# Two later norms by stream between halves of output tiles, and four modulation blocks on VectorE instead of TensorE

## The chip, the core and the metric

The kernel runs on one core of a Trainium2 chip. TensorE (PE in the profile) multiplies matrices into PSUM, VectorE (DVE) and ScalarE (ACT) work elementwise, and SyncE (SP) issues nearly all weight loads. The metric is the device time of one execution in microseconds (us).

## The reference

Two layers of a diffusion transformer on 256 latent tokens (stream 1) and 256 context tokens (stream 0), width 1024, in fp32. Every sublayer is "modulated norm, mixer, gated residual"; the six modulation vectors of a layer come from one conditioning vector for each stream.

```python
s_lat = jax.nn.silu(c)
s_ctx = jax.nn.silu(c_ctx)[None]
for l in range(DEPTH):
    sh_m, sc_m, g_m, sh_f, sc_f, g_f = jnp.split(s_lat @ w_mod[l] + b_mod[l], 6, axis=-1)
    csh_m, csc_m, cg_m, csh_f, csc_f, cg_f = jnp.split(s_ctx @ w_mod[l] + b_mod[l], 6, axis=-1)
    u = modulate(h, norm_mix[l], sh_m, sc_m)      # rms_norm(h) * (1 + scale) + shift
    uc = modulate(hc, norm_mix[l], csh_m, csc_m)
    ...   # y, yc = hybrid_mixer (l = 0) or ssd_mixer (l = 1)
    h = h + g_m[:, None] * y
    h = h + g_f[:, None] * conv_ffn(modulate(h, norm_ffn[l], sh_f, sc_f), ...)
    if need_ctx:      # layer 0 only
        hc = hc + cg_m[:, None] * yc
        hc = hc + cg_f[:, None] * conv_ffn(modulate(hc, norm_ffn[l], csh_f, csc_f), ...)
```

The hybrid mixer is a neighbourhood attention beside a gated linear recurrence (hgrn), then one output projection. The ssd mixer is a state-space scan with its own projections. `conv_ffn` is two up-projections, a convolution of width 3, a gelu gate and a down-projection.

## The kernel before

**Layout.** Activations lie as 128 features by 512 tokens: columns 0 to 255 are stream 0, 256 to 511 stream 1. `h` holds the residual in eight such tiles (k = 0 to 7). A matrix product is made of two fp32r pieces for each operand: `xhi` and `xlo` for the activations, `whi` and `wlo` for a weight. `mm3` (L141) issues three matmuls for each k, so a projection of 128 outputs (`proj`, L146) is 24 matmuls over eight k.

**Weights.** `wsplit` (L126) loads a 128x1024 block `raw` by SyncE, rounds it on ScalarE to `whi` (L135) and takes the rest on VectorE as `wlo` (L137). All three have four buffers. `behind` can tie the next splits behind given instructions.

**Modulations** are made in two ways. In *blocks* on TensorE (`mod_block`, L187), eight matmuls for each block, at the end of a batch two transposes and a reduction (`mod_finish`, L199 to L201); `queue` and `fetch` load the next block, two tiles `wv`. In *units* on VectorE (`vec`, L269): a unit is one row block of 128 outputs, two `junk` operations over 128x1024 whose sum goes to `dots`, one for each stream. `vec_fetch` (L252) loads up to three units ahead, each into a tile `wv`. Units and blocks share the five buffers of `wv`. Eight units fill one of the six chunks of a layer.

**Stages.** `hybrid`: first norm, two recurrence pairs, `attention` (head pairs: scores L684 and L685 on PE, bias L689, row maximum L691, exponent on ScalarE, reciprocal L694 and scaling L695 on VectorE, transposes L698, values L704, then `mhi`, `mlo` at L397 and L398), output projection `wo0` of eight tiles n (the last in two stream halves), each with `residual` (L390, `h`) and `sumsq` (L313 `nsq`, L317 `nacc`). Its products over k = 4 to 7 need `xhi`, `xlo`, those over k = 0 to 3 need `mhi`, `mlo`. Then `ffn(0)`: `norm_mod`, 22 features f with projections a (`ps_a`) and v (`ps_s`), in three chunks each followed by eight down-projection tiles m, the last again in halves. Layer 1: `norm_mod`, `ssd` (projections, L837 to L1010), `ffn(1)` on stream 1 alone.

**A later norm** (`norm_mod`, L381) issues a block, the sums over partitions (L324), a block, the rsqrt chain (`rsv` L328, Ln and Exp on ScalarE L288, `rst` L330 and L331, `nr` L332), the broadcast (L340), a block, and then for each k and stream `nt` (L374, VectorE), `xhi` (L376, ScalarE), `xlo` (L377, VectorE).

**What sets the order.** The code gives dependences and a program order; a list scheduler then fixes the instruction order of each engine at build time, from a model of its own. An engine executes its instructions in that order. Moving code in one place can so move instructions of other stages.

Of the kernel before, what the change touches and what calls it, by code (L numbers as in the profile page):

```python
# [43 lines left out]
class Net:  # L44
# [274 lines left out]
    def norm_r(self, ps, t0, n, meanwhile):  # L319
# [5 lines left out]
        between = meanwhile(last)  # L325
        r = self.w.tile([P, 4], F32, tag="nr", bufs=1, name=self.nm("nr"))[:, :nt]
# [6 lines left out]
        if not self.ps0:  # L333
            self.behind = [(self.squared, done.ins), (), (), ()]
# [7 lines left out]
        meanwhile(last)  # L342
# [24 lines left out]
    def norm_u(self, l, which, k, r, xhi, xlo, streams, pool):  # L367

        nc = self.nc
        t = pool.tile([P, T], F32, tag="nt", bufs=2, name=self.nm("nt"))  # L370
# [41 lines left out]
    def ffn(self, l, streams, xhi, xlo, last):  # L412
# [3 lines left out]
        with tc.tile_pool(name=f"ffn{l}", bufs=1) as p:  # L416
            self.norm_mod(l, 1, xhi, xlo, streams, p)
            for c, (f0, nf) in enumerate(FF_CHUNKS):
                hh = p.tile([P, NK, n], F32R, tag="hh", name=self.nm("hh"))
                hl = p.tile([P, NK, n], F32R, tag="hl", name=self.nm("hl"))  # L420
                for j in range(nf):
                    f = f0 + j
                    pa, pv = self.ps_a()[:, :n], self.ps_s()[:, :n]
                    self.proj(pa, self.i["wup"][l, f], xhi, xlo, toks=toks)
                    self.proj(pv, self.i["wup"][l, NFF + f], xhi, xlo, toks=toks)
                    if f == 1:
                        self.flush()
# [7 lines left out]
                for m in range(NK):  # L435
                    final = not last and c == len(FF_CHUNKS) - 1

                    for part in ((st,) for st in streams) if final and m == NK - 1 else (streams,):
                        o = (part[0] - streams[0]) * S
                        ps = self.ps_a()[:, :S * len(part)]  # L440
                        if part[0] == streams[0]:
                            w = self.wsplit(self.i["wdn"][l, m, :, f0:f0 + nf], [P, nf, P])
# [682 lines left out]
```

## Time and profile before

| | us |
|---|---|
| median of three runs (lowest to highest) | 1235.34 (1234.79 to 1238.77) |
| the profiled execution | 1236.18 |
| its span in the trace | 1234.4 |
| PE busy | 1205.3 (98%) |
| VectorE busy | 924.7 (75%) |
| ScalarE busy | 589.8 (48%) |

The profiled execution has 1.78 us around its span. Stages in the trace, us from its start: recurrence to about 210, attention to 335, output projection to 363.5, ffn(0) from 370.3 to 740, ssd to 1038, ffn(1) to the end. A busy share of PE counts pipelined matmuls one behind the other; what matters is when the next one starts. The granted clock is 1.00 in the stretches shown below.

### The profile page before, as it was taken

The numbers are of one execution on the slowest core, as the hardware profiler recorded it, in microseconds if no ns is written. First come the engines' busy times: TensorE is split into PE (matmuls) and PEld (weight loads), VectorE is DVE, ScalarE is ACT, GpSimd is POOL, SyncE is SP. The second block draws the span as 40 slices with busy tenths as digits, with TensorE's granted clock in tenths as the row PEclk, the third lists the DMA queues.
The fourth block names the chain that finished last, engine by engine and source line by source line (L and its number), as shares of the span: only waits on it lengthen the run. The fifth ranks groups of instructions, "written<-read, shape, count | busy, mean of one in ns | idle before, by whom it ended". The sixth has DMA issues, their size and how long they took to land.

```text
span 1234.4 us, 19131 instructions
## 1 busy us (share of the span) xinstructions
PE 1205.3 (98%) x7519; PEld 981.4 (80%) x7519; DVE 924.7 (75%) x1596; ACT 589.8 (48%) x915; POOL 0.2 (0%) x4
## 2 busy tenths in 40 slices
PE   5999999999999999999999999999999999999998
PEld 3687787766678888888888887878777798999998
DVE  4799999777569999984344457598989786766675
ACT  4554545787545331233133336556363644645452
POOL 0000000000000000000000000000000000000000
PEclk9999999999999999999999999999999999999999
DMA  9852636313055667762323233445344245565663
GB/s 375 311 180 74 221 102 175 129 56 124 13 161 183 204 217 223 222 201 76 111 91 96 83 112 130 151 144 171 104 152 129 93 135 156 182 186 181 189 183 106
DMA packets 55097, 189.35 MB, mean 153 GB/s; under 512 B 7136, under 2 KB 10848, under 8 KB 53728
## 3 DMA queue, kind: packets, MB, share of 16 engines
q1 hardware_dynamic: 51984, 185.17, 47.0%
q10 hardware_dynamic: 3024, 2.97, 0.8%
q8 instruction: 59, 0.97, 0.3%
q14 instruction: 30, 0.25, 0.1%
HBM read 187.00 MB, written 1.11 MB: 152 GB/s over the span
## 4 chain that ended last, share of the span: by engine, by line
PE 85%; DVE 6%; issue 2%; ACT 1%; DMA 0%; DVEq 0%; ACTq 0%
PE a L144 51%; PE s L144 16%; PE b L704 1%; PE s L161 1%; PE s L162 1%; PE s L163 1%; DVE junk L269 1%; PE b L997 1%; PE b L970 1%; PE b L1002 1%; DVE Q L519 1%; PE s L684 1%; PE b L698 1%; PE s L685 1%; DVE K L519 1%
## 5 line engine op out<-in xcount | busy, mean ns | idle before, releaser
L135 ACT CAST whi<-raw 128x1024 fp32r<-128x1024 f32 (+1 forms) x234 | 241.0, 1032 | 345.3 <-PE a L144 276.9
L137 DVE TENSOR_TENSOR wlo<-raw,whi 128x1024 fp32r<-128x1024 f32 (+1 forms) x234 | 280.5, 1199 | 101.4 <-ACT whi L135 99.8
L144 PE MATMUL a<-xhi,wlo 128*128 128x512 f32 (+1 forms) x740 | 268.9, 370 | 3.6 <-ACT va L639 1.9
L144 PE MATMUL a<-xhi,whi 128*128 128x512 f32 (+1 forms) x740 | 270.8, 366 | 0.0
L144 PE MATMUL a<-xlo,whi 128*128 128x512 f32 (+1 forms) x740 | 258.7, 367 | 2.8 <-DVE xlo L377 2.8
L144 PEld LDWEIGHTS a<-xhi,wlo 128*128 128x128 f32 x740 | 139.0, 188 | 31.3 <-issue 4.1
L144 PEld LDWEIGHTS a<-xlo,whi 128*128 128x128 f32 x740 | 137.4, 188 | 31.5 <-issue 4.6
L144 PEld LDWEIGHTS a<-xhi,whi 128*128 128x128 f32 x740 | 139.3, 188 | 24.7 <-issue 2.9
L269 DVE SCALAR_TENSOR_TENSOR junk<-wv,rows 128x1024 f32<-128x1024 f32 x128 | 156.2, 1221 | 1.9
L144 PE MATMUL s<-xhi,wlo 128*128 128x512 f32 (+1 forms) x376 | 128.4, 341 | 0.0
L144 PE MATMUL s<-xhi,whi 128*128 128x512 f32 (+1 forms) x376 | 128.2, 341 | 0.0
L144 PE MATMUL s<-xlo,whi 128*128 128x512 f32 (+1 forms) x376 | 121.5, 341 | 0.0
L144 PE MATMUL a<-hh,whi 128*128 128x256 f32 (+1 forms) x359 | 120.1, 335 | 0.0
L144 PE MATMUL a<-hh,wlo 128*128 128x256 f32 (+1 forms) x359 | 113.1, 335 | 0.0
L144 PE MATMUL a<-hl,whi 128*128 128x256 f32 (+1 forms) x359 | 112.5, 336 | 0.0
L390 DVE SCALAR_TENSOR_TENSOR h<-a,modT,h 128x256 f32<-128x256 f32 x90 | 40.7, 480 | 69.5 <-PE a L144 69.4
L144 PEld LDWEIGHTS s<-xhi,wlo 128*128 128x128 f32 x376 | 70.5, 188 | 9.5 <-issue 0.4
L144 PEld LDWEIGHTS s<-xhi,whi 128*128 128x128 f32 x376 | 70.6, 188 | 9.5 <-issue 0.4
L144 PEld LDWEIGHTS s<-xlo,whi 128*128 128x128 f32 x376 | 69.2, 188 | 9.0
L144 PEld LDWEIGHTS a<-hh,whi 128*128 128x128 f32 x359 | 67.5, 188 | 7.7
L144 PEld LDWEIGHTS a<-hl,whi 128*128 128x128 f32 x359 | 65.7, 188 | 8.2 <-DVE hl L398 0.5
L144 PEld LDWEIGHTS a<-hh,wlo 128*128 128x128 f32 x359 | 66.0, 188 | 7.8
(339 smaller groups left out, 1793.9 us busy)
## 6 DMA issues: line engine op xcount, KB each, us to landing
raw<-in_wup SPq DMA_DIRECT2D x88, 512.0 KB, 4.0
wv<-in_wmodT SPq DMA_DIRECT2D x64, 512.0 KB, 4.4
raw<-in_win SPq DMA_DIRECT2D x41, 512.0 KB, 3.8
raw<-in_wdn SPq DMA_DIRECT2D x32, 448.0 KB, 3.4
raw<-in_wo SPq DMA_DIRECT2D x24, 512.0 KB, 3.7
wm<-in_wmod SPq DMA_DIRECT2D x8, 1024.0 KB, 10.9
wv<-in_wmod SPq DMA_DIRECT2D x16, 512.0 KB, 4.4
raw<-in_wdn SPq DMA_DIRECT2D x16, 512.0 KB, 3.7
```

The source lines that it names most:

```text
L135: nc.scalar.copy(hi, raw)
L137: nc.vector.tensor_tensor(out=lo, in0=raw, in1=hi.bitcast(F32), op=ALU.subtract)
L144: self.last_mm = self.nc.tensor.matmul(ps, w, x, start=(first and i == 0), stop=(last and i == 2))
L161: mm(ps, xhi[:, k, tok], wlo[:, kk, :], start=(k == 0), stop=False)
L162: mm(ps, xhi[:, k, tok], whi[:, kk, :], start=False, stop=False)
L163: mm(ps, xlo[:, k, tok], whi[:, kk, :], start=False, stop=(k == NK - 1))
L269: nc.vector.scalar_tensor_tensor(out=self.junk, in0=w, scalar=1.0, in1=self.rows[:, s], op0=ALU.mult, op1=ALU.mult, accum_out=self.dots[:, ...
L390: self.nc.vector.scalar_tensor_tensor(out=self.h[:, n, s * S:(s + 1) * S], in0=ps[:, off:off + S], scalar=self.mod(l, chunk, n, s), in1=se ...
L519: mul = lambda o, t: nc.vector.tensor_tensor(out=o, in0=o, in1=t, op=ALU.mult)
L684: nc.tensor.matmul(ps, qs[rows, e, tok], kl[rows, :w], start=True, stop=False)
L685: nc.tensor.matmul(ps, qs[:, e, tok], ks[:, e, :w], start=False, stop=True)
L698: nc.tensor.transpose(pt[:, b * P:(b + 1) * P], pr[:, b * P:(b + 1) * P], self.ident)
```

## The change

Three things change, and the modulations computed are the same.

1. In `wo0` and in the last chunk of ffn(0), tiles 6 and 7 are both taken by stream: 6 and 7 of stream 0, the norm of stream 0 (`norm_stream`), 6 and 7 of stream 1, the norm of stream 1. The first four projections behind (f = 0, 1 of ffn(0)) or the first two (`wdt` and `win1[16]` of ssd) are taken as stream 0 of all and then stream 1 of all (`proj_streams`), as matmuls of 256 columns.
2. Chunk 2 of layer 1 is added to the vector units: 48 units (with those before, 144 `junk`) in place of 40 (128). Of the eight TensorE blocks four remain; they are queued at the end of ssd and run in the norm of ffn(1) (three) and at f = 1 there; the transposes of the last come at f = 2.
3. With no block in a norm, `behind` ties the first two weight splits after a stream's norm to nothing and the third and fourth to its `nr`.

```diff
@@ -331,7 +331,8 @@
         nc.vector.tensor_tensor(out=t, in0=t, in1=v, op=ALU.mult)
         done = nc.vector.scalar_tensor_tensor(out=r, in0=t, scalar=1.5, in1=r, op0=ALU.add, op1=ALU.mult)
         if not self.ps0:
-            self.behind = [(self.squared, done.ins), (), (), ()]
+            late = (self.squared, done.ins)
+            self.behind = [late, (), (), ()] if meanwhile else [late, late, (), ()]
         prs = [self.ps_b()[:, :S] for _ in range(nt // 2)] if self.ps0 else [self.ps_b()[:, :n]]
         with self.after([between] if between else ()):
             for b in range(nt):
...
@@ -378,6 +380,20 @@
                                            op0=ALU.add, op1=ALU.subtract)
         return u
 
+    def norm_stream(self, l, which, st, xhi, xlo):
+
+        r = self.norm_r(self.ps_b(), st * S, S, None)
+        for k in range(NK):
+            self.norm_u(l, which, k, r, xhi, xlo, (st,), self.w)
+
+    def proj_streams(self, jobs, xhi, xlo):
+
+        splits = [self.wsplit(src, [P, NK, P]) for _, src in jobs]
+        for st in STREAMS:
+            t = slice(st * S, (st + 1) * S)
+            for (ps, _), w in zip(jobs, splits):
+                self.proj(ps[:, t], None, xhi, xlo, toks=t, split=w)
+
     def norm_mod(self, l, which, xhi, xlo, streams, pool):
         self.bg(1, self.last_mm)
         r = self.norm_r(self.ps_s(), S * streams[0], S * len(streams), lambda i: self.bg(1, i))
...
@@ -414,17 +430,25 @@
         n = S * len(streams)
         toks = slice(streams[0] * S, (streams[-1] + 1) * S)
         with tc.tile_pool(name=f"ffn{l}", bufs=1) as p:
-            self.norm_mod(l, 1, xhi, xlo, streams, p)
+            if last:
+                self.norm_mod(l, 1, xhi, xlo, streams, p)
             for c, (f0, nf) in enumerate(FF_CHUNKS):
                 hh = p.tile([P, NK, n], F32R, tag="hh", name=self.nm("hh"))
                 hl = p.tile([P, NK, n], F32R, tag="hl", name=self.nm("hl"))
                 for j in range(nf):
                     f = f0 + j
-                    pa, pv = self.ps_a()[:, :n], self.ps_s()[:, :n]
-                    self.proj(pa, self.i["wup"][l, f], xhi, xlo, toks=toks)
-                    self.proj(pv, self.i["wup"][l, NFF + f], xhi, xlo, toks=toks)
-                    if f == 1:
-                        self.flush()
+                    if f == 0 and not last:
+                        early = [(self.ps_a(), self.ps_s()) for _ in (0, 1)]
+                        self.proj_streams([(ps, self.i["wup"][l, NFF * i + ff]) for ff, pss in enumerate(early)
+                                           for i, ps in enumerate(pss)], xhi, xlo)
+                    if f < 2 and not last:
+                        pa, pv = early[f]
+                    else:
+                        pa, pv = self.ps_a()[:, :n], self.ps_s()[:, :n]
+                        self.proj(pa, self.i["wup"][l, f], xhi, xlo, toks=toks)
+                        self.proj(pv, self.i["wup"][l, NFF + f], xhi, xlo, toks=toks)
+                    if f in (1, 2) and last:
+                        self.bg(1, self.last_mm)
                     if not last:
                         self.vec(1)
                     t = p.tile([P, n], F32, tag="t", bufs=2, name=self.nm("t"))
...
@@ -432,18 +456,22 @@
                     nc.scalar.activation(t, t, AF.Gelu_apprx_tanh)
                     nc.vector.tensor_tensor(out=t, in0=t, in1=pv, op=ALU.mult)
                     self.split_to(hh[:, j, :], hl[:, j, :], t)
-                for m in range(NK):
-                    final = not last and c == len(FF_CHUNKS) - 1
-
-                    for part in ((st,) for st in streams) if final and m == NK - 1 else (streams,):
-                        o = (part[0] - streams[0]) * S
-                        ps = self.ps_a()[:, :S * len(part)]
-                        if part[0] == streams[0]:
-                            w = self.wsplit(self.i["wdn"][l, m, :, f0:f0 + nf], [P, nf, P])
-                        self.proj(ps, None, hh, hl, nk=nf, toks=slice(o, o + S * len(part)), split=w)
-                        self.residual(l, 5, m, ps, part, final)
+                final = not last and c == len(FF_CHUNKS) - 1
+                ws = {}
+                whole = [(m, streams) for m in range(NK - 2 if final else NK)]
+                for m, part in whole + ([(m, (st,)) for st in streams for m in (6, 7)] if final else []):
+                    if m not in ws:
+                        ws[m] = self.ps_a()[:, :n], self.wsplit(self.i["wdn"][l, m, :, f0:f0 + nf], [P, nf, P])
+                    ps, w = ws[m]
+                    o = slice((part[0] - streams[0]) * S, (part[-1] + 1 - streams[0]) * S)
+                    self.proj(ps[:, o], None, hh, hl, nk=nf, toks=o, split=w)
+                    self.residual(l, 5, m, ps[:, o], part, final)
                     if not last:
                         self.vec(1)
+                    if final and m == 5:
+                        self.vec(NK * 6)
+                    if final and m == NK - 1:
+                        self.norm_stream(1, 0, part[0], xhi, xlo)
                     if last and c == len(FF_CHUNKS) - 1:
                         nc.scalar.dma_start(self.out[:, m, :], self.h[:, m, S:T])
 
...
@@ -767,17 +795,19 @@
                 self.split_to(xhi[:, i], xlo[:, i], self.h[:, i])
             nc.sync.dma_start(self.h, self.i["xT"])
             self.vec(NK * 3)
-            self.vec_queue([(0, 5), (1, 0), (1, 1), (1, 3), (1, 4)])
-            self.queue([(1, 1, 0, 3), (1, 1, 3, 1), (1, 1, 4, 2), (1, 1, 6, 2)])
-            for n in range(NK):
-                whi, wlo = self.wsplit(self.i["wo0"][n], [P, NK, P])
-                for part in ((0,), (1,)) if n == NK - 1 else (STREAMS,):
-                    toks = slice(part[0] * S, (part[-1] + 1) * S)
-                    ps = (self.ps_s() if n in (3, 4) else self.ps_a())[:, :S * len(part)]
-                    for c, k in enumerate((4, 5, 6, 7, 0, 1, 2, 3)):
-                        hi, lo = (xhi, xlo) if k >= 4 else (mhi, mlo)
-                        self.mm3(ps, whi[:, k], wlo[:, k], hi[:, k, toks], lo[:, k, toks], c == 0, c == 7)
-                    self.residual(0, 2, n, ps, part, True)
+            self.vec_queue([(0, 5), (1, 0), (1, 1), (1, 2), (1, 3), (1, 4)])
+            ws = {}
+            for n, part in [(n, STREAMS) for n in range(NK - 2)] + [(n, (st,)) for st in STREAMS for n in (6, 7)]:
+                if n not in ws:
+                    ws[n] = (self.ps_s() if n in (3, 4) else self.ps_a(), *self.wsplit(self.i["wo0"][n], [P, NK, P]))
+                toks = slice(part[0] * S, (part[-1] + 1) * S)
+                ps, whi, wlo = ws[n]
+                for c, k in enumerate((4, 5, 6, 7, 0, 1, 2, 3)):
+                    hi, lo = (xhi, xlo) if k >= 4 else (mhi, mlo)
+                    self.mm3(ps[:, toks], whi[:, k], wlo[:, k], hi[:, k, toks], lo[:, k, toks], c == 0, c == 7)
+                self.residual(0, 2, n, ps[:, toks], part, True)
+                if n == NK - 1:
+                    self.norm_stream(0, 1, part[0], xhi, xlo)
 
 
     def ssd(self, xhi, xlo):
...
@@ -785,12 +815,14 @@
         with ExitStack() as es:
             keep = es.enter_context(tc.tile_pool(name="dec", bufs=1))
             p = es.enter_context(tc.tile_pool(name="ssd", bufs=1))
-            dec, sums = self.ssd_decays(xhi, xlo, keep, p)
+            early = [self.ps_a() for _ in (0, 1)]
+            self.proj_streams([(early[0], self.i["wdt"]), (early[1], self.i["win1"][16])], xhi, xlo)
+            dec, sums = self.ssd_decays(early[0], keep, p)
             yhi = p.tile([P, 16, S], F32R, name="yhi")
             ylo = p.tile([P, 16, S], F32R, name="ylo")
             for g in range(4):
-                self.ssd_group(g, xhi, xlo, p, dec, yhi, ylo, sums if g == 0 else None)
-                self.flush()
+                self.ssd_group(g, xhi, xlo, p, dec, yhi, ylo, *((early[1], sums) if g == 0 else ()))
+            self.queue([(1, 1, 4, 2), (1, 1, 6, 2)])
 
             acc = {}
             for n, b in [(n, b) for b in (0, 1) for n in range(5)] + [(n, b) for n in range(5, NK) for b in (0, 1)]:
```

**Where the order moves: VectorE at the end of attention.** `pr` is a softmax tile, `s` its scores, `sm` its row sums; `mlo<-b_3174` is the last one of attention. Before:

```order
L695 TENSOR_SCALAR pr_3109<-pr_3109,sm_3107 128x512
L689 TENSOR_TENSOR s_3138<-s_3138,bias_3141 128x256
L694 RECIPROCAL sm_3125<-sm_3125 128x1
L691 TENSOR_REDUCE sm_3144<-s_3138 128x1
L695 TENSOR_SCALAR pr_3127<-pr_3127,sm_3125 128x512
L689 TENSOR_TENSOR s_3156<-s_3156,bias_3159 128x256
L691 TENSOR_REDUCE sm_3162<-s_3156 128x1
L694 RECIPROCAL sm_3144<-sm_3144 128x1
L695 TENSOR_SCALAR pr_3146<-pr_3146,sm_3144 128x512
L694 RECIPROCAL sm_3162<-sm_3162 128x1
L695 TENSOR_SCALAR pr_3164<-pr_3164,sm_3162 128x512
L398 TENSOR_TENSOR mlo<-b_3174,mhi 128x256
```

In the changed kernel (a view of the same place, from behind the reciprocal that `pr_3127` needs):

```order
L269 SCALAR_TENSOR_TENSOR junk,dots_4366<-wv_4443,rows 128x1024
L723 TENSOR_SCALAR pr_3127<-pr_3127,sm_3125 128x512
L719 TENSOR_REDUCE sm_3144<-s_3138 128x1
L717 TENSOR_TENSOR s_3156<-s_3156,bias_3159 128x256
L269 SCALAR_TENSOR_TENSOR junk,dots_4366<-wv_4480,rows 128x1024
L722 RECIPROCAL sm_3144<-sm_3144 128x1
L719 TENSOR_REDUCE sm_3162<-s_3156 128x1
L723 TENSOR_SCALAR pr_3146<-pr_3146,sm_3144 128x512
L269 SCALAR_TENSOR_TENSOR junk,dots_4366<-wv_4480,rows 128x1024
L722 RECIPROCAL sm_3162<-sm_3162 128x1
L269 SCALAR_TENSOR_TENSOR junk,dots_4366<-wv_4517,rows 128x1024
L723 TENSOR_SCALAR pr_3164<-pr_3164,sm_3162 128x512
```

Four `junk` have come between the operations of the last three softmax tiles.

**VectorE at the start of the output projection.** `h` is a residual, `wlo` a weight split. Before, behind the last `mlo`:

```order
L390 SCALAR_TENSOR_TENSOR h<-a_3210,modT,h 128x256 x2
L390 SCALAR_TENSOR_TENSOR h<-a_3245,modT,h 128x256 x2
L390 SCALAR_TENSOR_TENSOR h<-a_3281,modT,h 128x256 x2
L137 TENSOR_TENSOR wlo_3350<-raw_3347,whi_3349 128x1024
L317 TENSOR_TENSOR nacc_3237<-nacc_3237,nsq_3272 128x512
L137 TENSOR_TENSOR wlo_3387<-raw_3384,whi_3386 128x1024
```

In the changed kernel, behind the last `mlo`:

```order
L269 SCALAR_TENSOR_TENSOR junk,dots_4695<-wv_4591,rows 128x1024
L406 SCALAR_TENSOR_TENSOR h<-a_3200,modT,h 128x256 x2
L406 SCALAR_TENSOR_TENSOR h<-a_3235,modT,h 128x256 x2
L406 SCALAR_TENSOR_TENSOR h<-a_3271,modT,h 128x256 x2
L317 TENSOR_TENSOR nacc_3233<-nacc_3233,nsq_3268 128x512
L406 SCALAR_TENSOR_TENSOR h<-s_3307,modT,h 128x256 x2
L137 TENSOR_TENSOR wlo_3347<-raw_3344,whi_3346 128x1024
L317 TENSOR_TENSOR nacc_3233<-nacc_3233,nsq_3304 128x512
L137 TENSOR_TENSOR wlo_3384<-raw_3381,whi_3383 128x1024
```

A `junk` stands ahead of the first residual, and the next weight split (`wlo_3347`, tile 4) is behind four pairs of residuals instead of three.

**PE at the same place.** `s_3343` is output tile 4, `a_3380` tile 5, `a_3416` and `a_3451` are tiles 6 and 7. In the changed kernel:

```order
L144 MATMUL s_3307<-mhi,whi_3310 128x512
L144 MATMUL s_3307<-mhi,wlo_3311 128x512
L144 MATMUL s_3343<-xlo,whi_3346 128x512
L144 MATMUL s_3343<-xhi,whi_3346 128x512
L144 MATMUL a_3380<-xlo,whi_3383 128x512
L144 MATMUL a_3380<-xhi,whi_3383 128x512
L144 MATMUL a_3416<-xlo,whi_3419 128x256
L144 MATMUL a_3416<-xhi,whi_3419 128x256
L144 MATMUL a_3451<-xlo,whi_3454 128x256
L144 MATMUL a_3451<-xhi,whi_3454 128x256
L144 MATMUL s_3343<-xhi,wlo_3347 128x512
L144 MATMUL s_3343<-xlo,whi_3346 128x512
```

Matmuls with `wlo` come behind eight that need `whi` alone. Before, at the place where the three waiting tiles are done, PE goes on with tile 3 (`s_3317`, its first of 15):

```order
L144 MATMUL a_3281<-mlo,whi_3277 128x512
L144 MATMUL a_3281<-mhi,whi_3277 128x512
L144 MATMUL a_3281<-mhi,wlo_3278 128x512
L144 MATMUL s_3317<-xlo,whi_3313 128x512
L144 MATMUL s_3317<-xhi,whi_3313 128x512
L144 MATMUL s_3317<-xhi,wlo_3314 128x512
L144 MATMUL s_3317<-mlo,whi_3313 128x512
L144 MATMUL s_3317<-mhi,whi_3313 128x512
```

**VectorE at the first later norm.** `rsv`, `rst` and `nr` are the small steps of the rsqrt chain, `nt` the first product with the norm. Before:

```order
L390 SCALAR_TENSOR_TENSOR h<-a_3491,modT,h 128x256
L317 TENSOR_TENSOR nacc_3237<-nacc_3237,nsq_3517 128x256
L328 TENSOR_SCALAR rsv_3556<-s_3538 128x4
L330 TENSOR_TENSOR rst_3557<-nr_3555 128x4
L331 TENSOR_TENSOR rst_3557<-rst_3557,rsv_3556 128x4
L332 SCALAR_TENSOR_TENSOR nr_3555<-rst_3557,nr_3555 128x4
L137 TENSOR_TENSOR wlo_3751<-raw_3748,whi_3750 128x1024
L374 SCALAR_TENSOR_TENSOR nt_3583<-h,A,b_3564 128x256 x2
```

In the changed kernel, for stream 0:

```order
L317 TENSOR_TENSOR nacc_3233<-nacc_3233,nsq_3483 128x256
L406 SCALAR_TENSOR_TENSOR h<-a_3416,modT,h 128x256
L328 TENSOR_SCALAR rsv_3490<-b_3486 128x2
L269 SCALAR_TENSOR_TENSOR junk,dots_4695<-wv_4772,rows 128x1024
L330 TENSOR_TENSOR rst_3491<-nr_3489 128x2
L317 TENSOR_TENSOR nacc_3233<-nacc_3233,nsq_3558 128x256
L331 TENSOR_TENSOR rst_3491<-rst_3491,rsv_3490 128x2
L269 SCALAR_TENSOR_TENSOR junk,dots_4695<-wv_4846,rows 128x1024
L332 SCALAR_TENSOR_TENSOR nr_3489<-rst_3491,nr_3489 128x2
L406 SCALAR_TENSOR_TENSOR h<-a_3451,modT,h 128x256
L269 SCALAR_TENSOR_TENSOR junk,dots_4695<-wv_4846,rows 128x1024
L376 SCALAR_TENSOR_TENSOR nt_3501<-h,A,b_3498 128x256
```

Three `junk` of this piece stand between the sum of squares and the first `nt`, among the small steps.

## Rows read from the trace of the kernel before

**Rows 1.** The page, parts 1, 4, 5 and 6.

```profile
PE 1205.3 (98%) x7519; PEld 981.4 (80%) x7519; DVE 924.7 (75%) x1596; ACT 589.8 (48%) x915; POOL 0.2 (0%) x4
...
PE 85%; DVE 6%; issue 2%; ACT 1%; DMA 0%; DVEq 0%; ACTq 0%
...
L269 DVE SCALAR_TENSOR_TENSOR junk<-wv,rows 128x1024 f32<-128x1024 f32 x128 | 156.2, 1221 | 1.9
...
wv<-in_wmod SPq DMA_DIRECT2D x16, 512.0 KB, 4.4
```

**Rows 2.** Windows: length, then busy us (instructions) of each engine, clock, DMA.

```profile
225.00:335.00 110.00, 109.78 (x487) 70.11 (x487) 76.93 (x170) 81.11 (x175) 0.00 (x0) 1.00 0.22 72
335.00:363.50 28.50, 28.50 (x147) 23.99 (x145) 18.74 (x30) 12.96 (x16) 0.00 (x0) 1.00 0.41 129
363.50:370.30 6.80, 5.92 (x69) 3.50 (x67) 4.41 (x12) 3.20 (x8) 0.00 (x0) 1.00 0.58 187
```

**Rows 3.** Timeline of PE, tiles 6 and 7 and first projection: start, duration.

```profile
352.26 0.40 PE L144 MATMUL a<-xlo,whi 128*128 128x512 f32 x1
...
357.86 0.28 PE L144 MATMUL a<-xlo,whi 128*128 128x256 f32 x1
...
363.40 0.28 PE L144 MATMUL a<-mhi,wlo 128*128 128x256 f32 x1
...
370.27 0.50 PE L144 MATMUL a<-xhi,wlo 128*128 128x512 f32 x1
```

**Rows 4.** Timeline of VectorE, first later norm, from residual to nr.

```profile
363.72 0.48 DVE L390 SCALAR_TENSOR_TENSOR h<-a,modT,h 128x256 f32<-128x256 f32 x1 [1.38 <-PE a L144]
...
366.99 0.16 DVE L332 SCALAR_TENSOR_TENSOR nr<-rst,nr 128x4 f32<-128x4 f32 x1
```

**Rows 5.** Timeline of PE, second later norm (in brackets idle time and releaser).

```profile
739.93 0.28 PE L144 MATMUL a<-hh,wlo 128*128 128x256 f32 x1
...
762.62 0.50 PE L144 MATMUL a<-xhi,wlo 128*128 128x512 f32 x1 [0.37 <-ACT wx L837]
```

**Rows 6.** Timeline of PE, third later norm.

```profile
1040.35 1.07 PE L187 MATMUL b<-wv,silu_c 128*32 128x256 f32 x16
...
1042.34 0.38 PE L199 MATMUL b<-c_ident,mrow 128*128 128x128 f32 x2
1044.00 0.38 PE L144 MATMUL a<-xhi,wlo 128*128 128x256 f32 x1 [1.28 <-ACT xhi L376]
```

**Rows 7.** Timeline of VectorE, end of attention, start of the output projection.

```profile
324.33 0.41 DVE L398 TENSOR_TENSOR mlo<-b,mhi 128x256 fp32r<-128x256 f32 x1
324.66 0.48 DVE L695 TENSOR_SCALAR pr<-pr,sm 128x512 f32<-128x512 f32 x1
325.05 0.42 DVE L689 TENSOR_TENSOR s<-s,bias 128x256 f32<-128x256 f32 x1
325.39 0.15 DVE L694 RECIPROCAL sm<-sm 128x1 f32<-128x1 f32 x1
325.51 0.69 DVE L691 TENSOR_REDUCE sm<-s 128x1 f32<-128x512 f32 x1
326.12 0.48 DVE L695 TENSOR_SCALAR pr<-pr,sm 128x512 f32<-128x512 f32 x1
...
334.73 0.42 DVE L398 TENSOR_TENSOR mlo<-b,mhi 128x256 fp32r<-128x256 f32 x1 [4.33 <-ACT mhi L397]
336.37 2.44 DVE L390 SCALAR_TENSOR_TENSOR h<-a,modT,h 128x256 f32<-128x256 f32 x6 [1.22 <-PE a L144]
338.73 1.21 DVE L137 TENSOR_TENSOR wlo<-raw,whi 128x1024 fp32r<-128x1024 f32 x1
```

**Rows 8.** Timeline of VectorE, last unit before attention and first one behind.

```profile
221.23 1.22 DVE L269 SCALAR_TENSOR_TENSOR junk<-wv,rows 128x1024 f32<-128x1024 f32 x1
...
381.01 1.22 DVE L269 SCALAR_TENSOR_TENSOR junk<-wv,rows 128x1024 f32<-128x1024 f32 x1
...
382.15 0.48 DVE L377 SCALAR_TENSOR_TENSOR xlo<-nt,modT,xhi 128x256 fp32r<-128x256 f32 x1
```

More of the change, by code (lines that the diff above doesn't have):

```diff
@@ L324, in norm_r @@
             last = nc.tensor.matmul(ps[:, b:b + 1], self.acc[:, t0 + b * P:t0 + (b + 1) * P], self.ones[:, 0:1], start=True, stop=True)
-        between = meanwhile(last)
-        r = self.w.tile([P, 4], F32, tag="nr", bufs=1, name=self.nm("nr"))[:, :nt]
+        between = meanwhile(last) if meanwhile else None
+        r = self.w.tile([P, 4], F32, tag="nr", bufs=2, name=self.nm("nr"))[:, :nt]
         v, t = (self.w.tile([P, 4], F32, tag=g, bufs=1, name=self.nm(g))[:, :nt] for g in ("rsv", "rst"))
@@ L341, in norm_r @@
                                         start=True, stop=True)
-        meanwhile(last)
+        if meanwhile:
+            meanwhile(last)
         return prs if self.ps0 else prs[0]
@@ L369, in norm_u @@
         nc = self.nc
-        t = pool.tile([P, T], F32, tag="nt", bufs=2, name=self.nm("nt"))
+        t = pool.tile([P, S * len(streams)], F32, tag="nt", bufs=2 if pool is not self.w else 3, name=self.nm("nt"))
         for i, s in enumerate(streams):
@@ L802, in ssd, with ssd_decays @@
                     self.residual(1, 2, n, acc[n], (1,), True)
-    def ssd_decays(self, xhi, xlo, keep_pool, p):
+    def ssd_decays(self, ps, keep_pool, p):
         nc = self.nc
@@ L827, in ssd_decays @@
         MID_F, MID_B, LE, GE, GT, LT = range(6)
-        ps = self.ps_a()
-        self.proj(ps, self.i["wdt"], xhi, xlo)
         bias, alog = self.small[:, 3:4], self.small[:, 4:5]
@@ L910, in ssd_decays, with ssd_group @@
         return d, sums
-    def ssd_group(self, g, xhi, xlo, p, d, yhi, ylo, before=None):
+    def ssd_group(self, g, xhi, xlo, p, d, yhi, ylo, early=None, before=None):
         nc = self.nc
@@ L925, in ssd_group @@
             n, toks = (S, slice(S, T)) if i == 1 else (T, slice(0, T))
-            ps = self.ps_a()[:, :n]
-            self.proj(ps, win[idx], xhi, xlo, toks=toks)
+            ps = early
+            if i or not early:
+                ps = self.ps_a()[:, :n]
+                self.proj(ps, win[idx], xhi, xlo, toks=toks)
             dst = (BT, CT)[i] if i < 2 else tl([P, T], "xf", 2)
@@ L1027, in run @@
         self.ffn(0, STREAMS, xhi, xlo, False)
-        self.vec(NK * 5)
-        self.flush()
-        with self.tc.tile_pool(name="nm1", bufs=1) as p:
-            self.norm_mod(1, 0, xhi, xlo, STREAMS, p)
         self.ssd(xhi, xlo)
```

## Prediction

> **What bounds the kernel now.** I read the page first: TensorE (PE) is busy 98% of the span and carries 85% of the chain that ended last, VectorE (DVE) 6% [rows 1]. So a change pays only by closing holes in PE, or by taking work off it; it costs wherever it makes PE wait. The windows then say where holes are: 0.2 us in attention (225 to 335 us), none in the output projection (335 to 363.5), 0.88 us at the first later norm [rows 2]. A norm is nevertheless dear: between the last output matmul at 363.40 and the first projection at 370.27 PE does 6.87 us of sums, broadcasts and modulation blocks, most of which only fill the wait for the norm's chain [rows 3]. The same windows give VectorE's room: 33 of 110 us idle in attention, 10 of 28.5 in the output projection, and almost none at a norm's end.
>
> **What is removed and added on PE.** Four of eight modulation blocks go, 16 records and 1.07 us each [rows 6], with their transposes: about 4.5 us of work, but it stood in norm gaps. Halving tiles costs nothing by itself: tile 6 of 512 columns starts its 24 matmuls over 5.60 us (352.26 to 357.86), tile 7 in halves takes 47 steps from 357.86 to 363.40, 0.118 us each, against 0.233 for twice the columns [rows 3].
> The Trainium skill, "TensorE: Matmul & The Clock Gate", section "Back-to-back issue gap", speaks against halves: the spacing of weight load and matmul pairs is 81 ns at 128 columns and 131 ns at 512, so about 98 ns at 256 (an estimate between them), 1.49 times the work for two halves. The halves measured here do not follow it.
>
> **What is moved on VectorE, and why it matters.** Eight vector units more run as 16 `junk` operations, 1.22 us each [rows 1]. The larger effect is not in the diff: the vector units share the five wv buffers with the TensorE blocks, and without those loads ahead of them their own start early. Before, no `junk` runs between 221.23 and 381.01 us [rows 8]. In the new order 28 stand between the middle of attention and its last `mlo`, 7 more before the first norm's rsqrt, 4 between that and the second stream's (39 x 1.15 = 45 us, at the 1.14 us from one start to the next start in [rows 8]). VectorE runs in order, so what stands behind one waits for it. The 28 ask 32 us of the 33 that were idle: their sum fits, their places decide.
>
> (a) *Mid-attention* (24 of the 28). By stretches of the new order I summed VectorE's and PE's own work; in six of seven VectorE stays within 0.6 us of PE or well under it. Bounds: 0 to 4 us. I take 1, because PE has projection matmuls as filler there.
>
> (b) *End of attention.* From one `mlo` on, VectorE has `mlo` 0.33, four scalings 0.39 (two measure up to 0.49), two bias additions 0.34, three reciprocals 0.12, two reductions 0.61, by starts [rows 7]: about 4.4 us, and now four `junk` among them, 4.6 more. The last softmax scaling ends 9.0 us after `mlo` begins, about 9.6 after the matmuls that feed `mlo`; its transposes follow at 9.8. PE's own work up to there is three score matmuls, three sets of transposes and 17 projection matmuls at 0.233: some 7.2 us, an estimate with 1.1 us a set for transposes and the scores ahead of it. So 2.65 us of hole. Before, the same place had VectorE idle for 4.33 us before the next `mlo`, and no hole in PE [rows 7]. Bounds: 0 (PE late by that much anyway) to 4.6 (all four on the path). I take 2.65.
>
> (c) *Start of the output projection.* Before, PE still had 15 matmuls of tile 3 left after the three waiting tiles when VectorE split the next weight (`wlo` at 338.73) [rows 7]. Now 17 of tile 3 are spent during (b), and PE has 18 x 0.233 + 4 x 0.118 = 4.7 us until it needs that `wlo`. VectorE reaches the end of it after `mlo` (at 0.9), one `junk` 1.15, four pairs of `h` at 0.8 [rows 7], one `nacc` 0.6, `wlo` 1.2: 7.1 us. Hole 2.4 to 2.5. Bounds: 0 to 3.6 (one more `junk`'s length). I take 2.5.
>
> (d) *First later norm.* I count from the last matmul of tile 7, stream 0. In the order before that point is 363.40 - 5.60 = 357.80; the first projection (370.27) is 12.5 us behind it, and four projections of 24 matmuls at 0.233 end 34.9 behind it [rows 3]. In the changed order PE covers 5.6 us with tiles 6 and 7 of stream 1. Stream 0's chain from `h` to `nr` takes 3.27 us before [rows 4], which would hide; but eight `junk` stand in it and its sequel. One ahead of the `nacc`, one before each of two small steps: `nr` comes at 6.8, the broadcast at 7.1, one more `junk` before the first `nt`, first projection at 9.6. Stream 0's share, held to VectorE's 0.39 a step, ends near 17.8; two more `junk` lie ahead of stream 1's `nr`, ready at 19.4, and the third weight's `wlo` is tied behind it. The last 144 half matmuls follow, 16.8 us: 36.3. That is 1.4 us worse than before. Without `junk` on the path (about 5.8 us of the eight) the same sum ends 4.5 us better. I take +1.4; bounds -4.5 to +3.
>
> (e) *Second norm.* No `junk` is left there. The old order's last matmul starts at 739.93; less 42 half matmuls at 0.118 that is 735.0, and the group of projections behind the first starts at 762.62, 27.6 us later [rows 5]. Now two halves of stream 1 cover the chain of stream 0, its projections that of stream 1, and the same group starts 25.3 behind: 4.9 of halves, 11.2 of the two early projections, 2.8 of the short one behind them, 1.2 of sums and broadcasts, and 5.2 of waits (0.9 for stream 0's first `xhi`, the rest for VectorE's steps of 0.39 and a buffer). So -2.25. Bounds -5.5 (three blocks, transposes and both waits all gone) to 0.
>
> (f) *Third norm and ffn(1).* A third block stands now before its first projection, in a 1.28 us wait for `xhi` [rows 6]; its second load is issued about 1039 and lands in 4.4 us by the page's median [rows 1]: 0 to +1, I take 0.3. The fourth block (1.0) and its transposes (0.4 [rows 6]) lie in packed projections: +1.4, nothing hides it.
>
> **Sum**: 1 + 2.65 + 2.5 + 1.4 - 2.25 + 0.3 + 1.4 = +7.0 us. The profiled execution takes 1236.18 (span 1234.4 and 1.78 around it), 0.84 above the median 1235.34; +7 on the median is 1242.3, so I forecast 1242.
>
> **Rivals.**
> 1. *The streams pay as drawn* (faster). If VectorE lags PE by less than I walked, (a) to (c) vanish and the `junk` in (d) fall into waits for ScalarE: -4.5 - 2.25 + 0.3 + 1.4 = -5, so 1230. For it: VectorE had room for every one of the 28 by sum. Against it: strict order, and `junk` between two dependent small steps of `nr`. It decides if the first broadcast comes within 5.6 us of tile 7's first half.
> 2. *It cancels* (same). The holes (b) and (c) hide because PE's real work before them runs later than I count, but (d) stands: +1.4 - 2.25 + 0.3 + 1.4 = +0.85, so 1236. Half of (b) and (c) still gives 1238.7, the edge of "same".
> 3. *Attention becomes bound by VectorE* (much slower). In (b) a `junk` costs 0.66 us each (2.65 by four). If half of the other 24 cost that, (a) is 8 instead of 1: 1249.
> 4. *Weight loads bind the halves.* 120 matmuls at the first norm and 69 at the second are split, 189 x 0.233 = 44 us; at 1.49 times that is +21 on top of rival 2, 1257. That ratio is the estimate from the page named above; the rows' 0.118 against 0.233 exclude it nearly.
>
> **How the numbers follow.** Chances: forecast 0.48, rival 1 0.17, rival 2 0.25, rival 3 0.09, rival 4 0.01. A measurement can tell about 0.3%, 3.7 us, from no change. The forecast's own range, from its bounds taken together, is 1239 to 1247. Rival 2 lies wholly in "same", and a little of the forecast's low end; rival 1 is faster but for its weaker half. Faster 0.16, same 0.28, slower 0.56. The range 1230 to 1248 leaves out about one in ten at either end.
>
> **What the profile of the changed kernel would show.** For (b): PE idle on the transposes of the last head pair, VectorE named, 2 to 3 us, and `junk` without idle time between. For (c): a wait of PE for `wlo` some 5 us after the last attention matmul, about 2.5 us over at most three waits. For (d): the first projection 9 to 10 us after tile 7's first half, and a wait for a broadcast or `wlo` some 8 us later. For (e): the next group of ssd projections about 25 us after stream 0's end, with no L187 before it. For (f): L187 among projections of ffn(1). I am wrong if PE's holes from 225 to 363 us sum to under 2 us (then rivals 1 or 2), or to over 10 (rival 3).

## The result, and the profile after

The changed kernel takes 1243.31 us (median of 5 runs, 1241.36 to 1246.85) against 1236.03 for the kernel before in the same comparison: 1.0057 times as long, 95% interval 1.0036 to 1.0078. The forecast was 1242. The experiments show that two effects stand behind this number, and that the prediction had seen only one, at half its size: the new order costs 15 to 17 us, and the weight buffers, which the change moved by 32 bytes, give back 8 to 10. They move by a line of the change that the diff above leaves out: the small tile `nr` has two buffers instead of one.

The page's first part, and windows (length, busy us and instructions of each engine, granted clock, DMA share, GB/s) of the changed kernel:

```profile
PE 1201.6 (97%) x7640; PEld 996.4 (80%) x7640; DVE 939.0 (76%) x1635; ACT 588.6 (47%) x919; POOL 0.2 (0%) x4
```

```profile
225.00:335.00 110.00, 104.50 (x453) 66.24 (x452) 95.96 (x210) 77.63 (x169) 0.00 (x0) 0.99 0.39 121
335.00:363.50 28.50, 26.70 (x126) 20.13 (x125) 25.73 (x46) 13.07 (x18) 0.00 (x0) 0.96 0.51 170
...
333.80:337.20 3.40, 2.84 (x7) 2.28 (x8) 3.36 (x9) 1.29 (x4) 0.00 (x0) 0.51 0.27 106
...
378.10:381.50 3.40, 3.40 (x17) 3.40 (x17) 3.40 (x9) 1.66 (x5) 0.00 (x0) 0.52 0.00 0
```

Against [rows 2]: VectorE's idle time in attention fell from 33 us to 14, and PE, which had 0.2 us of holes from 225 to 363.5, now has 5.5 + 1.8 = 7.3. Behind the holes at the end of attention PE ran 3.4 us at a granted clock of 0.51, the lower of its two levels (1.2 of 2.4 GHz), and so again behind a hole at the first norm. The holes at the end of attention, in PE's timeline (start, duration, in brackets idle time and releaser):

```profile
330.19 0.50 PE L712 MATMUL s<-kl,qs 64*128 64x512 f32 x1 [0.72 <-ACT pr L721]
...
332.38 0.63 PE L726 MATMUL b<-c_ident,pr 128*128 128x128 f32 x4 [0.87 <-DVE pr L723]
...
334.36 0.80 PE L144 MATMUL s<-xlo,whi 128*128 128x512 f32 x1 [1.35 <-ACT pr L721]
```

The transposes at 332.38 wait for a softmax tile. The other two matmuls write a tile `s`, and wait until ScalarE has made `pr` from the scores that lay there; the one at 334.36 is the first of the projection matmuls that the prediction took as PE's filler. VectorE's timeline of the same stretch:

```profile
330.62 1.21 DVE L269 SCALAR_TENSOR_TENSOR junk<-wv,rows 128x1024 f32<-128x1024 f32 x1
...
331.75 0.48 DVE L723 TENSOR_SCALAR pr<-pr,sm 128x512 f32<-128x512 f32 x1
332.15 0.68 DVE L719 TENSOR_REDUCE sm<-s 128x1 f32<-128x512 f32 x1
```

The scaling that the transposes at 332.38 wait for stands behind a `junk`. ScalarE's copy of these transposes stands in turn ahead of the `pr` that the matmul at 334.36 waits for:

```profile
333.05 0.58 ACT L727 COPY pT<-b 128x512 f32<-128x512 f32 x1 [1.10 <-PE b L726]
...
333.53 0.69 ACT L721 ACTIVATE pr<-s,sm 128x512 f32<-128x512 f32 x1
```

So 2.2 of the 2.9 us go back to that `junk`. The first wait, 0.72, ends with a `pr` that ScalarE starts at 329.35, right behind an `mhi` for whose input from PE it had waited 1.63 us. The holes at the start of the output projection:

```profile
349.60 0.39 PE L144 MATMUL a<-xlo,whi 128*128 128x256 f32 x1 [0.82 <-ACT whi L135]
...
350.55 0.38 PE L144 MATMUL a<-xlo,whi 128*128 128x256 f32 x1 [0.44 <-ACT whi L135]
...
351.31 0.50 PE L144 MATMUL s<-xhi,wlo 128*128 128x512 f32 x1 [0.26 <-DVE wlo L137]
```

At the first later norm the chain that ended last runs through `junk` itself (start, length, what):

```profile
370.17 0.35 PE b L324 x4
370.54 0.16 DVE rsv L328
370.70 1.14 DVE junk L269 x2
371.84 0.07 DVE rst L330
371.91 0.34 DVE nacc L317
372.32 1.14 DVE junk L269 x2
373.46 0.07 DVE nr L332
...
374.29 1.98 ACT whi L135 x2
376.27 0.42 ACT xhi L378
```

Three steps of 0.07 to 0.16 us are pulled 3 us apart by two `junk`; then, which the prediction did not see, two weight splits stand ahead of the first `xhi` on ScalarE. PE's timeline there, from the first half tile of stream 1 to the end of the four projections:

```profile
366.80 0.28 PE L144 MATMUL a<-xlo,whi 128*128 128x256 f32 x1
...
373.60 0.71 PE L341 MATMUL b<-c_ident,nr 128*128 128x128 f32 x4 [0.49 <-DVE nr L332]
376.73 0.39 PE L144 MATMUL a<-xhi,wlo 128*128 128x256 f32 x1 [2.43 <-ACT xhi L378]
...
403.45 0.40 PE L144 MATMUL a<-xhi,wlo 128*128 128x512 f32 x1
```

### The profile page after: what moved, and what is told of

The parts are those of the page before. It is cut to its first block, busy times and chain, and to the rows that moved or that the text cites. A ratio compares the mean times of both kernels' runs of the same rounds, so it can differ in the third digit from the quotient of the medians.

```text
span 1242.8 us, 19423 instructions
## 1 busy us (share of the span) xinstructions
PE 1201.6 (97%) x7640; PEld 996.4 (80%) x7640; DVE 939.0 (76%) x1635; ACT 588.6 (47%) x919; POOL 0.2 (0%) x4
## 4 chain that ended last, share of the span: by engine, by line
PE 82%; DVE 10%; ACT 3%; issue 2%; DMA 2%; SPq 0%; DVEq 0%; ACTq 0%
PE a L144 48%; PE s L144 16%; DVE junk L269 2%; DVE wlo L137 1%; PE b L732 1%; PE b L1029 1%; PE b L1002 1%; DVE Q L547 1%; PE b L1034 1%; ACT whi L135 1%; PE s L163 1%; PE s L161 1%; PE s L162 1%; DVE K L547 1%; PE s L712 1%
## 5 line engine op out<-in xcount | busy, mean ns | idle before, releaser
L144 PE MATMUL a<-xhi,whi 128*128 128x512 f32 (+1 forms) x776 | 277.2, 358 | 0.0
L269 DVE SCALAR_TENSOR_TENSOR junk<-wv,rows 128x1024 f32<-128x1024 f32 x144 | 175.6, 1219 | 1.7
L144 PEld LDWEIGHTS a<-xhi,wlo 128*128 128x128 f32 x776 | 147.1, 190 | 31.2 <-issue 4.6
L144 PEld LDWEIGHTS a<-xlo,whi 128*128 128x128 f32 x776 | 145.2, 190 | 30.0 <-issue 4.2
L144 PEld LDWEIGHTS a<-xhi,whi 128*128 128x128 f32 x776 | 147.6, 190 | 20.9 <-issue 3.3
L144 PE MATMUL s<-xhi,wlo 128*128 128x256 f32 (+1 forms) x392 | 131.2, 335 | 0.3 <-DVE wlo L137 0.3
L144 PE MATMUL s<-xhi,whi 128*128 128x256 f32 (+1 forms) x392 | 131.3, 335 | 0.0
L144 PE MATMUL s<-xlo,whi 128*128 128x256 f32 (+1 forms) x392 | 124.8, 336 | 1.4 <-ACT pr L721 1.4
L406 DVE SCALAR_TENSOR_TENSOR h<-a,modT,h 128x256 f32<-128x256 f32 x90 | 40.9, 480 | 63.8 <-PE a L144 63.8
L144 PEld LDWEIGHTS s<-xhi,wlo 128*128 128x128 f32 x392 | 75.0, 191 | 7.7 <-DVE wlo L137 0.5
L144 PEld LDWEIGHTS s<-xlo,whi 128*128 128x128 f32 x392 | 73.7, 192 | 8.8 <-ACT pr L721 1.6
```

The costliest lines, as they stand in the source:

```text
L144: self.last_mm = self.nc.tensor.matmul(ps, w, x, start=(first and i == 0), stop=(last and i == 2))
L269: nc.vector.scalar_tensor_tensor(out=self.junk, in0=w, scalar=1.0, in1=self.rows[:, s], op0=ALU.mult, op1=ALU.mult, accum_out=self.dots[:, ...
L406: self.nc.vector.scalar_tensor_tensor(out=self.h[:, n, s * S:(s + 1) * S], in0=ps[:, off:off + S], scalar=self.mod(l, chunk, n, s), in1=se ...
```

## The experiments

Each kernel was compared with the kernel before on the same chip, but for the control; ratios are to that kernel. Its medians in these comparisons lie between 1235.27 and 1236.38 us, so a difference in us between kernels of two comparisons can be off by 1.

**Control.**

> The kernel before once more, for a profile taken on the same chip as the next three. Its median was 1235.34 and its 24 matmuls of 512 columns took 5.60 us; in the profile of the changed kernel they took about 5.46, and 24 of 256 columns 2.87 instead of 2.82. If that belongs to the chip or the run, the profile of before shows the same steps here as the next three kernels; if it belongs to the change, before keeps 5.60 and the next three show about 5.46.

One run took 1233.29 us, its span is 1231.5. The steps stayed those of before, although two kernels with streams on the same chip had the other ones. So the step goes with the kernel.

**Units held back.** In `vec` each `junk` is ordered behind `hold`, which the last `xlo` of the first later norm sets behind the loop over the tiles of `wo0`; `FREE` holds the first three units of (0, 5).

```diff
             for s in STREAMS:
+                with self.after([self.hold] if self.hold and (l, c, k) not in FREE else ()):
...
+            self.hold = self.last_xlo
```

> The changed kernel with the vector units of ffn(0), but for the first three, ordered behind the last xlo of the first later norm; nothing else is moved. Theory (the junk of the early units make the holes): the 6.2 us of holes at the end of attention and in the output projection go, with the 1 in mid-attention, and the first norm comes out 4.5 us better than before instead of 1.4 worse: about 13 us under the changed kernel, 1230 to 1232, below before. Rival (the streams themselves cost, the units were hidden): the time stays at 1240 to 1244. In between: 1236 to 1239, if the held units only move the holes into ffn(0).

Measured 1232.24 us, 0.9976 (0.9963 to 0.9989): 11 us under the changed kernel (10 by the ratios), where the theory had 13. No `junk` stands in attention, and PE has 0.33 us of holes from 225 to 335. But one term did not come: the first norm. PE's timeline and a window of this kernel:

```profile
370.65 1.00 PE L347 MATMUL b<-c_ident,nr 128*128 128x128 f32 x4 [2.26 <-DVE nr L338]
```

```profile
370.90:374.30 3.40, 3.36 (x16) 3.06 (x16) 3.35 (x8) 1.31 (x3) 0.00 (x0) 0.50 0.43 140
```

With no `junk` in the way PE still waits 2.26 us for the second stream's `nr`, and then runs 3.4 us at half clock.

**All units held** (no unit free).

> As the run with held units, but with all units of ffn(0) behind the last xlo of the first later norm: the six junk that both kernels have at the end of the recurrence (205 to 222 us, where VectorE is nearly saturated) go into ffn(0) too. Theory: if VectorE sets the pace there, up to 6 x 1.15 = 7 us less than the run with held units, 1224 to 1231; if PE or the chain does, the same time as that run.

1234.54 us, 0.9988 (0.9978 to 0.9998), not below the run before it: no gain is seen from moving the six `junk` at the end of the recurrence.

**Held to the end of attention alone** (`hold` is the last `mlo` of attention).

> The changed kernel with the same units held behind the last mlo of attention alone: they may start in the output projection and the first later norm (14 junk there by the order, 11 in the changed kernel). Theory (the holes of attention are the units' cost, at its end above all): the last mlo comes about 110.5 us behind attention's start instead of 121.6, and the time lies at 1234 to 1237, with 2 to 4 us left of junk in the output projection and norm. Rival (output projection and norm carry the loss): 1239 to 1243.

1234.39 us, 0.9992 (0.9981 to 1.0004). The last `mlo` is back at 110.5 us behind attention's start. So about 9 of the 11 us (8 of 10 by the ratios) belong to units in attention.

**Modulations alone.** The kernel before with chunk 2 added to the units, the four blocks queued behind ssd, norms whole.

> The kernel before with the modulations alone moved (144 junk, four TensorE blocks in the third norm and in ffn(1)); both later norms taken whole as before. Theory: the units start in attention here too, so the holes of attention and output projection stay (6 to 9 us), the first norm gets junk among its steps and loses its blocks (0 to +2), ffn(1) pays 1.7: 1243 to 1248. Rival (the loss comes from the streams): within 2 us of before, 1236 to 1238.

1255.87 us, 1.0178 (1.0158 to 1.0197): worse than the theory's upper end. The waits in attention are those of the changed kernel; the surplus is mostly in the norms, where no block and no half tile now fills the chain. Waits of PE at the first norm (total, times, longest), and windows there and at the second:

```profile
PE b L340 <- DVE nr L332: 4.4, 1, 4.4
PE s L324 <- DVE nacc L317: 1.9, 1, 1.9
PE a L144 <- ACT xhi L376: 1.5, 1, 1.5
```

```profile
374.00:387.60 13.60, 7.84 (x22) 6.32 (x23) 13.60 (x34) 4.39 (x11) 0.00 (x0) 0.51 0.46 159
...
756.30:766.50 10.20, 7.48 (x23) 6.18 (x24) 8.53 (x23) 4.40 (x11) 0.00 (x0) 0.51 0.17 51
```

Here the low clock lasts 13.6 and 10.2 us, where the kernel before has 1.00. The weight buffers of this kernel lie where those of before lie, so it stands beside the changed kernel without the shift (1253.53 us, 1.0140, below): taking the norms by stream is not where the loss comes from, and by these ratios it gives a little of it back.

**The address of the weight buffers.** `nr` with two buffers in the kernel before; every engine's order is unchanged.

```diff
-        r = self.w.tile([P, 4], F32, tag="nr", bufs=1, name=self.nm("nr"))[:, :nt]
+        r = self.w.tile([P, 4], F32, tag="nr", bufs=2, name=self.nm("nr"))[:, :nt]
```

> The kernel before with one number changed: the small tile nr has two buffers instead of one, as in the changed kernel. The instructions and their order are the same as before on every engine; the weight buffers and all that lies behind them move up by 32 bytes, to where they lie in the changed kernel. In the profiles so far the products of xhi and xlo step by 0.2333 us at 512 columns and 0.1168 at 256 in kernels without the shift, 0.2275 and 0.1198 with it. Theory (the address sets the step): 2220 matmuls by -0.0059 and 1176 by +0.0030, -13.1 + 3.5 = -9.6, so about 1226. Rival (the step belongs to the streams or to the order): no difference, 1234 to 1237.

1228.73 us, 0.9939 (0.9925 to 0.9953). The theory held, 1.9 us short of its -9.6. PE's timeline, first matmuls of successive projections (24 lie between two rows of a pair), of the control:

```profile
390.56 0.39 PE L144 MATMUL a<-xhi,wlo 128*128 128x512 f32 x1
396.15 0.39 PE L144 MATMUL s<-xhi,wlo 128*128 128x512 f32 x1
...
1112.03 0.28 PE L144 MATMUL s<-xhi,wlo 128*128 128x256 f32 x1
1114.83 0.28 PE L144 MATMUL a<-xhi,wlo 128*128 128x256 f32 x1
```

and of the kernel with the shift alone:

```profile
389.76 0.39 PE L144 MATMUL a<-xhi,wlo 128*128 128x512 f32 x1
395.20 0.39 PE L144 MATMUL s<-xhi,wlo 128*128 128x512 f32 x1
...
1102.00 0.28 PE L144 MATMUL a<-xhi,wlo 128*128 128x256 f32 x1
1104.87 0.28 PE L144 MATMUL s<-xhi,wlo 128*128 128x256 f32 x1
```

5.59 becomes 5.44 for 24 of 512 columns, 2.80 becomes 2.87 for 24 of 256.

**The shift taken from the held and the changed kernel** (`bufs=3` for `nr`).

> The run with held units with a third buffer of nr: the same order on PE and VectorE, the weight buffers 32 bytes further, 64 above those of before. Theory (the place within 64 bytes sets the step): the steps are those of before again, 2064 x 0.0059 - 1488 x 0.0030 = +7.7 over the held run's 1232, about 1240; the streams and moved modulations as such then make the kernel some 4 us slower than before. Rival: same as the held run, 1230 to 1234.

1240.70 us, 1.0033 (1.0021 to 1.0045): as the theory said. So even with the units held, the change makes the kernel slower at the addresses of before. The wait for the second stream's `nr` is as long as in the held kernel, but the clock behind it stayed up:

```profile
370.44 0.68 PE L347 MATMUL b<-c_ident,nr 128*128 128x128 f32 x4 [2.26 <-DVE nr L338]
```

```profile
370.70:374.10 3.40, 3.04 (x26) 2.85 (x26) 3.40 (x8) 1.31 (x3) 0.00 (x0) 1.00 0.46 140
```

> The changed kernel with a third buffer of nr, order unchanged. Theory: 1243.3 + 7.7 = 1251, which would be what the new order costs without the shift of the addresses: +15 over before, of which the units in attention, output projection and first norm make 11. Rival: 1242 to 1245.

1253.53 us, 1.0140 (1.0122 to 1.0159), 2.5 us above the theory. The changed order costs 17 us at that address. In the profile there is one stretch of 3.4 us at the low clock more than in the changed kernel, from 352.4 us, in the output projection; whether it makes the 2.5 us is not shown.

**Everything moved by 32 bytes.** An unused tile of 32 bytes ahead of all others.

> The kernel before with 32 unused bytes ahead of everything: xhi, xlo and h move up by 32 bytes too, not the weight buffers and what lies behind them alone; order unchanged. The shift of the weight buffers alone gave 1228.7 (0.9939 of before). Theory A (the address of the weights itself counts): steps of 0.2275 and 0.1198 for the products of xhi and xlo, about 1229. Theory B (the place of the weights relative to xhi and xlo counts): 0.2332 and 0.1168 as before, 1235 to 1237.

1235.07 us, 1.0005 (0.9993 to 1.0017), steps as before (5.60 in the timeline):

```profile
390.53 0.40 PE L145 MATMUL a<-xhi,wlo 128*128 128x512 f32 x1
396.13 0.40 PE L145 MATMUL s<-xhi,wlo 128*128 128x512 f32 x1
```

This is what theory B forecast. The weight buffers lie where they lie in the kernel with the shift alone, and the step is the old one: the weights' own address does not set it, and the place of something that did not move there counts too. That it is a distance is the simplest reading, not shown.

**Other weight buffers in ffn(1).** `ring` is the pool of ffn(1), 32 bytes off, with `tag="whi"` and `"wlo"` from it.

> The kernel with the shift alone, and whi and wlo of ffn(1) in buffers of their own that lie 32 bytes off a multiple of 64 like those of before (raw stays). Theory (the address of whi and wlo sets the step, and 256 columns go better where 512 go worse): the 1056 products of xhi and xlo in ffn(1) step by 0.1168 instead of 0.1199, -3.3, about 1225.5. Rival (another buffer's address, raw or a residual, sets it): 0.1199 and 1228 to 1229. The four more buffers could let splits run further ahead; PE waits too little in ffn(1) for that to show.

1233.37 us, 0.9982 (0.9972 to 0.9992). The rival held: the step stayed 2.88 us for 24. So in ffn(1) it is not the place of `whi` and `wlo` against `xhi` and `xlo` that sets it.

```profile
1109.90 0.28 PE L147 MATMUL s<-xhi,wlo 128*128 128x256 f32 x1
1112.78 0.28 PE L147 MATMUL a<-xhi,wlo 128*128 128x256 f32 x1
```

It lost nearly 5 us against the shift alone, around the third norm, where PE waited 1.7 us for `nacc` and the mean clock from 1030 to 1050 us was 0.83.

**Two blocks in the second norm.** The held kernel with a block behind each stream's broadcast there (`bg(1, ...)` in `norm_stream`) and none left in ffn(1).

> The run with held units, and two of the four TensorE blocks moved into the second norm (one behind each stream's broadcast), the other two in the third norm as before; nothing is left in ffn(1) and no third block in the third norm. In the held run PE waits there for a block's load for 1.9 us, and the block and transposes in ffn(1) take 1.4; in the second norm PE waits 1.1 for xhi, 0.6 for xlo and 1.3 for a buffer, which a block of 1.07 can fill in part. Theory: -1.9 - 1.4 + 0.5 to 1.5, so 1.8 to 2.8 under the held run, about 1230. Rival (the blocks delay the second norm by their full 2.5 us): 1231 to 1232.

1230.31 us, 0.9952 (0.9935 to 0.9969): 1.9 us under the held run, at the theory's low end (3.0 by the ratios); the intervals overlap, so the size is not settled.

**The second norm alone by stream.**

> The kernel before with the second norm alone taken by stream (tiles 6 and 7 of the last chunk in halves, wdt and win1[16] by stream, three blocks kept in that norm: one behind the first stream's broadcast, two behind the second's), the weight buffers 32 bytes up as in the kernel with the shift alone; first norm and units as before. Theory (streaming the second norm is worth the 2.3 us that stood in the prediction, less what the blocks do not hide): the group of projections behind the early ones 1 to 2 us earlier after stream 0's end, 1226.5 to 1228 against the 1228.7 of the shift alone. Rival (nothing is left: what the norm gains ssd's first group waits for later): 1228.5 to 1230.

1229.08 us, 0.9946 (0.9932 to 0.9959), the same as the shift alone: the rival. Between the last `hl` of ffn(0) and ssd's first `wx` it is 2.0 us faster (64.0 against 66.1), and ssd gives 1.5 back by its last `wx`, with a wait of PE that the shift alone does not have:

```profile
903.51 0.66 PE L960 MATMUL b<-c_ident,xf 128*128 128x128 f32 x4 [1.77 <-ACT xf L955]
```

## Why the prediction was right, and by which steps

The number was right by luck: the cost of the order was taken at half its size, and an effect that the sum did not have made up for the rest. The steps are sized against the kernel with the shift alone, whose weight buffers lie where those of the changed kernel lie. Starts of events on VectorE in us behind the first `rt` of attention (221.99, 222.70 and 221.43 in the three traces):

| event | shift alone | changed | held | changed minus shift |
|---|---|---|---|---|
| last `mlo` of attention | 110.5 | 121.6 | 110.5 | 11.1 |
| first `hl` of ffn(0) | 170.0 | 184.1 | 172.1 | 14.1 |
| last `hl` of ffn(0) | 471.4 | 484.4 | 472.4 | 13.0 |
| first `wx` of ssd | 537.4 | 548.1 | 536.1 | 10.7 |
| last `wx` of ssd | 760.6 | 774.2 | 760.3 | 13.6 |
| first `hl` of ffn(1) | 827.7 | 840.5 | 829.0 | 12.8 |
| end of the span | 1004.5 | 1020.1 | 1008.6 | 15.6 |

The sum of +7 stands against +15.6 here (+14.6 by the ratios, 1.0057 over 0.9939).

- **(a) to (c)**, predicted 6.15, were right in place and nearly in size: holes of 2.6 in mid-attention (predicted 1), 2.9 at its end (2.65) and 1.8 in the output projection (2.5), 7.3 in all. But the causes were only in part the predicted ones. At the end of attention only 0.87 us is a wait of transposes for VectorE; the rest is PE waiting for a tile `s` that ScalarE had still to read, 1.35 of it ahead of the very projection matmuls that the sum counted as filler. In the output projection 1.3 of the 1.8 us were waits for `whi` from ScalarE, not for `wlo`. And PE loses more than its holes: by the last matmul of tile 7, stream 0, as the prediction counts it, the changed kernel is 10.6 us behind the shift alone. The low clock, 0.51 for 3.4 us, makes at most 1.7 of the rest; some 2 us no row here names.
- **(d)**, walked by rows of the order, was right for the changed kernel: counted from the last matmul of tile 7, stream 0 (one step before 366.80), broadcast 6.9 us (predicted 7.1), first projection 10.0 (9.6), end of the four 36.8 (36.3). Its lower bound was wrong: without `junk` the norm was to be 4.5 us better than before, but the held kernel is 2.1 us later at the first `hl` than the shift alone, and without the shift it is level with the kernel before (171.2 against 171.1). The wait for the second stream's `nr` stands in place of the gain; at the shifted addresses the low clock behind it and the dearer halves come on top. So rival 1 had no ground even without the `junk`.
- **(e)**, predicted -2.25, measured 63.8 against 66.1 from the last `hl` to the first `wx`: -2.3. But ssd gave 2.9 us back by its last `wx` (226.1 against 223.2), at most 1.7 of them in a stretch of 3.4 us at a clock of 0.50 from 801.5; the run with that norm alone ended level.
- **(f)**, predicted +1.7: from ssd's last product of `yhi`, `ylo` to the ninth projection of ffn(1) PE takes 31.2 us against 29.1, +2.1, of which 0.7 lies ahead of the first projection (predicted 0.3); from there to the end both take 170.5. The rows are the predicted ones:

```profile
1047.22 0.64 PE L187 MATMUL b<-wv,silu_c 128*32 128x256 f32 x8 [0.83 <-DMA wv<-in_wmod]
...
1059.48 1.07 PE L187 MATMUL b<-wv,silu_c 128*32 128x256 f32 x16
```

- **The term that failed** is "halving tiles costs nothing" and, behind it, the silent one that the matmuls it does not touch keep their step. By [rows 3] two halves take the time of a whole; at the changed kernel's addresses a whole takes 0.2275 and a half 0.120, 5% more for two. Over 2064 wholes and 1488 halves of `xhi` and `xlo` that is 12.2 less and 4.5 more, -7.7; halving 156 wholes costs 1.9 of it, and the silent term, at the counts of before, gives 9.6 back. The held and the changed kernel rose by 8.5 and 10.2 when the shift was taken away (7.0 and 10.3 by the ratios). Rival 4, with its estimate of 49% more from "TensorE: Matmul & The Clock Gate", "Back-to-back issue gap" in the Trainium skill, stays far off.

The traces, not the total alone, exclude rivals 2 and 3: the holes are there, and mid-attention has 2.6 us of them, not 8.

## What to carry to other kernels

Work without dependences that a scheduler may hoist is not free on an engine with room: look where it lands, and tie it behind the last instruction of the stage that must not wait. Before crediting an edit with a gain, compare the step of an untouched inner loop in both traces; here it moved by 2.5% without a changed instruction. The fastest kernel measured is the one before with one spare buffer of a small tile, 1228.73 us, 0.9939; the second norm by stream on top of it, 1229.08, cannot be told from it.

## What the runs showed of the hardware that was not expected

- Moving the weight buffers and what lies behind them by 32 bytes against `xhi` and `xlo` changed 24 matmuls of 512 columns from 5.59 to 5.44 us and 24 of 256 from 2.80 to 2.87. Which pair of buffers matters stays open: moving `xhi` and `xlo` along undoes it, moving `whi` and `wlo` of ffn(1) elsewhere does not, and products of `hh` and `hl` keep 0.233 throughout.
- A wait of PE was often, not always, followed by the low clock, and then cost more than its length. After 2.26 us without work in the held kernel the granted clock was 0.50 for 3.4 us; the same wait in the same kernel without the shift was followed by 1.00. Around waits of 1.9 and 4.4 us in the run with the modulations alone it was 0.51 for 13.6. In ssd of the changed kernel it fell without a wait of PE ahead:

```profile
801.50:804.90 3.40, 3.40 (x9) 2.64 (x9) 1.56 (x4) 1.15 (x2) 0.00 (x0) 0.50 0.51 170
```

- With its blocks in the norms, the kernel before shows 1.00 at the first two later norms. Its waits there are shorter too, at most 0.5 us against 4.4, so that the blocks keep the clock up is likely and not shown.
